# P's diagonal blocks filled by ScalarE, attention's queries turned during retention, and a new entry into the MLP

## The chip, the cores and the metric

The kernel runs on one core of a Trainium2 chip. Its engines are TensorE (PE for the matmuls, PEld for the loading of their stationary operand), VectorE (DVE), ScalarE (ACT), GpSimd (POOL) and SyncE (SP, which here issues the DMAs). The metric is the device time of one execution in microseconds; the time before is the median of three runs.

## The reference, cut to what matters

One decoder layer over 16 meta tokens and 1024 tokens of 1024 channels, in float32:

```python
u = rmsnorm(h, norm1_w); proj = u @ w_in
y_ret = retention(...)            # 4 heads, chunks of 128 tokens, state carried from chunk to chunk
score = sum_h iw[h] * relu(iq[h] @ ik.T)          # indexer, causal
sel = top_k(score, 256)                           # keys that a query may see
logits = (rmsnorm(q) / 8) @ rmsnorm(k)[sel].T + rel_bias[t5_bucket(dist)]
y_dsa = softmax(logits) @ v[sel]                  # 8 heads of 64, keys and values shared
h = h + concat(y_ret, y_dsa) @ w_out
h = h + square(relu(rmsnorm(h, norm2_w) @ w_ff1)) @ w_ff2     # 4096 wide
```

## The kernel before

Products are made in split precision: an operand is kept as a rounded high part and the low part that is left, and a product takes three matmuls (high by high, low by high, high by low). A high part is a ScalarE copy, a low part a subtract of the high part from the source, on VectorE or GpSimd. Much of the work off TensorE is this splitting.

The program goes through these stages. First come norm, transposes and the indexer's scores, block by block of 128 tokens (to about 205 us). Then retention runs head by head, eight chunks each (`ret_in`, `ret_out`), while the thresholds of the top 256 are searched bit by bit: tiles 2 to 4 by counting on VectorE (L746), tiles 5 to 7 by a sum of signs on ScalarE (L751). When a threshold is known, `masks` turns a score tile into a mask on VectorE (L761 to L767). From about 410 to 607 us attention goes through sixteen units, a block of 128 queries and a half of the heads each: `attend_p` makes the logits and the exponentials, `attend_v` transposes them, splits them and multiplies them by the values, and the first half of the output projection is laid between the units (`out_piece`). The second half of the output projection follows, with the second norm (`norm2`) between its blocks, and from about 664 us the MLP, whose two products are done by a scheme of seven products for a two by two split (units m = 1 to 7 over operands U1 to U7; `unit1`, then `stage2`).

The order in which each engine gets its instructions is not that of the program text: a planner orders all instructions by program position and by when it believes their inputs and buffers to be there, so work of a later part fills gaps of an earlier one. PSUM has eight banks, three of tag A (`psA`) and five of tag R (`psB`).

What the change touches:

- `load_q(i)` (L554): loads the normed queries of block i, turns them by four transposes, and splits them into the tile `qs`, whose 128 partitions hold high and low parts of two heads by turns. It takes two ScalarE copies (L565) and two VectorE subtracts (L566) a block.
- `attend_v` (L607): the meta tokens' few columns of the exponentials go into `pm`, which is zero outside its diagonal blocks of 32 partitions. A ScalarE copy (L618) gives the high part `hi`, and four VectorE instructions (L621), one for each block of 32 partitions, write high or low parts into `pm`. One matmul (L638) reads `pm` at the end of the unit.
- `norm2` (L876): norm, eight transposes, and then the operands U2 and U4 (from blocks 0 to 3) or U3, U5, U6, U7 and the sum for U1 (from blocks 4 to 7), each split into halves; the low halves of U3, U4 and U6 are made by GpSimd (`halves`, L895).
- `prep1`, `unit1`, `EVAC`, `groups` (L944 to L1024): a unit of the MLP's first product is 12 matmuls of 512 columns into one PSUM bank; EVAC says into which sums its result goes. Units run in groups; a group is a slice p of the MLP's width and some of the seven m. The first groups are p = 1 with m = 2 and 4, all of p = 0, and the rest of p = 1.
- the loop over `todo` (L1143 to L1156): the last output block of the first half, then eight of the second, whose weights are loaded and split by `out_w(1)` ahead of the first of these.

Of the kernel before, what the change touches and what calls it, by code (L numbers as in the profile page):

```python
# [22 lines left out]
NB = 8  # L23
# [58 lines left out]
def layer(ctx, tc, x, meta, norm1_w, w_in, ret_w, q_w, k_w, rel, w_out, norm2_w, w1, w2,  # L82
# [361 lines left out]
    qd = dr.tile([128, NB, 512], F32, name="qd")  # L444

# [108 lines left out]
    def load_q(i):  # L554
        qr = wp.tile([128, 512], F32, tag="rl", name="qr", bufs=2)
        nc.sync.dma_start(qr, qd[:, i])
        tp = psA()
        for c in range(4):
            nc.tensor.transpose(tp[:, 128 * c:128 * c + 128], qr[:, 128 * c:128 * c + 128], ident)
        qst[i] = at["q"][:, i % 2]  # L560
        t4 = tp.rearrange("p (c n) -> p c n", c=4)
        q4 = qst[i].rearrange("p (c e) n -> p c e n", e=2)
        for e in range(2):
            a, z = (slice(0, 64), slice(64, 128)) if e == 0 else (slice(64, 128), slice(0, 64))
            nc.scalar.activation(q4[a, :, e], t4[a], AF.Copy)  # L565
            nc.vector.tensor_tensor(q4[z, :, e], t4[a], q4[a, :, e].bitcast(F32), op=ALU.subtract)  # L566

# [39 lines left out]
    def attend_v(i, g):  # L607
# [9 lines left out]
        hi = small.tile([128, 128], F32R, name="phm", tag="ytmp", bufs=1)  # L617
        nc.scalar.activation(hi, tp[:, :128], AF.Copy)  # L618
        for hh in range(4):
            z = slice(32 * hh, 32 * hh + 32)  # L620
            nc.vector.scalar_tensor_tensor(pm[z, hh], tp[z, :128], odd[z], hi[z].bitcast(F32),  # L621
                                           op0=ALU.mult, op1=ALU.subtract)
# [102 lines left out]
    for h in range(4):  # L725
        st["w", h] = load_cols(w_in, [(o + 128 * h, 128) for o in (RQ, RK, RV, RG)])
        ret_meta(h)
        for c in range(NB):
            if h == 3 and c == 5:
                open_att()  # L730
                load_q(0)
            if h == 3 and c == 6:
                load_q(1)
            if h == 3 and c == 7:
                spread((4, attend_p(0, 0)))
            cur = ret_in(h, c)
            if prev:
                ret_out(*prev)
            prev = cur
# [136 lines left out]
    def norm2(b, src, u):  # L876
# [15 lines left out]
        def halves(m, x, eng):  # L892
            h, l = [v[:, :, s] for v in U[m]]
            nc.scalar.activation(h, x, AF.Copy)
            eng.tensor_tensor(l, x, h.bitcast(F32), op=SUB)  # L895
# [3 lines left out]

        def total(m, x, y, op, eng):  # L900
            t = temp()
            nc.vector.tensor_tensor(t, x, y, op=op)
            halves(m, t, eng)
        g1, g2 = f1[0][:, b % 4], f1[1][:, b % 4]
        if b < 4:
            nc.scalar.activation(g1, tps[0], AF.Copy)
            halves(2, tps[0], nc.vector)
            nc.scalar.activation(g2, tps[1], AF.Copy)
            total(4, tps[1], g1, SUB, nc.gpsimd)
        else:  # L910
            t = temp()
            nc.scalar.activation(t, tps[0], AF.Copy)
            total(3, t, tps[1], SUB, nc.gpsimd)
            halves(5, tps[1], nc.vector)
            total(6, tps[0], g1, ADD, nc.gpsimd)
            total(7, tps[1], g2, ADD, nc.vector)
            nc.vector.tensor_tensor(g1, tps[1], g1, op=ADD)

# [27 lines left out]
    EVAC = {2: [("1b", 1), ("2b", -1)], 4: [("1b", "+"), ("1a", 1)], 3: [("2a", 1), ("2b", "+")], 5: [("2a", "+"), ("1a", "-")],  # L946
            6: [("2b", "+")], 7: [("1a", "+")], 1: [("1a", "+"), ("2b", "+")]}
    FIN = {("1b", 4), ("2a", 5), ("1a", 1), ("2b", 1)}
    ORD = (2, 4, 3, 5, 6, 7, 1)
    groups = [(1, ORD[:2]), (0, ORD), (1, ORD[2:])] + [(p, ORD) for p in range(2, NP)]  # L950
# [43 lines left out]
    def unit1(n):  # L994
# [10 lines left out]
        for q, how in EVAC[m]:  # L1005
            if how in (1, -1):
                tag, k = ("yd", 4) if q in ("1a", "2b") else ("aop", 6)
                C[p, q] = p2["p"].tile([128, 512], F32, tag=tag, name="c" + q, bufs=k)
                nc.scalar.activation(C[p, q], ps, AF.Copy, scale=float(how))
            else:  # L1010
                c = C[p, q]
                nc.vector.tensor_tensor(c, c, ps, op=ADD if how == "+" else SUB)
                if (q, m) in FIN:
                    nc.scalar.activation(c, c, AF.Relu)
                    nc.scalar.activation(c, c, AF.Square)
                    if q in HELD:
                        nc.sync.dma_start(hid[HELD[q]][:, p], c)
# [126 lines left out]
    pre = out_prep(*todo[0])  # L1144
    for k, (ch, b) in enumerate(todo):
        if k == 1:
            out_w(1, True)
        nxt = out_prep(*todo[k + 1]) if k < NB else None
# [5 lines left out]
        if k == 6:  # L1154
            w1_load(0, 0)
            w1_load(0, 1)  # L1156

    for n in range(2):
        prep1(n)
# [5 lines left out]
    for n in range(len(units)):  # L1165
# [4 lines left out]
        if 3 <= n < 7:  # L1170
            s = slice(128 * (n - 3), 128 * (n - 3) + 128)
            nc.scalar.activation(U[1][0][:, :, s], f1[0][:, n - 3], AF.Copy)
            nc.vector.tensor_tensor(U[1][1][:, :, s], f1[0][:, n - 3], U[1][0][:, :, s].bitcast(F32), op=SUB)
# [48 lines left out]
```

## Time and profile before

| | |
|---|---|
| median of 3 runs | 1297.18 us (1294.48 to 1297.89) |
| the profiled execution | 1296.34 us, its span 1294.6 us, mean granted TensorE clock 0.989 |
| busy, share of the span | PE 96%, PEld 79%, VectorE 79%, ScalarE 59%, GpSimd 17% |
| the chain that ended last | PE 69%, VectorE 19%, ScalarE 5%, issue 4%, DMA 2%, GpSimd 1% |

Busy time of PE counts each matmul from its start to its end, and matmuls overlap, so that a stretch in which PE is 90% busy can still hold much less than 90% of the matmuls that would fit. The chain is followed back from the last instruction to what released each; a share of it is time that nothing else hid.

### The profile page before, as it was taken

The page shows a single profiled execution, that of the slowest core. Times are in us where ns is not written, and L with a number is a line of the kernel's source. Part 1 is how long each engine was busy: PE and PEld are TensorE (multiplying, and loading weights), DVE is VectorE, ACT ScalarE, POOL GpSimd, SP SyncE. Part 2 cuts the span into 40 slices and gives each one's busy share as a digit, 9 for nine tenths or more (in the row PEclk, how much of TensorE's full clock was granted, in tenths as well). Part 3 has the DMA queues.
Part 4 walks back from the last instruction along what each step waited for, and adds up shares of the span by engine and source line. Part 5 has one row for each costly group of instructions (what it writes and reads, how often), then busy time and mean ns, then how long its engine had stood idle before and what let it go on. Part 6 is the DMA issues. An engine that isn't in the chain of part 4 may idle for free.

```text
span 1294.6 us, 18365 instructions
## 1 busy us (share of the span) xinstructions
PE 1240.1 (96%) x6032; PEld 1025.8 (79%) x6032; DVE 1022.2 (79%) x2298; ACT 757.9 (59%) x1612; POOL 221.1 (17%) x278
## 2 busy tenths in 40 slices
PE   5999989999999899999898999999999999999998
PEld 4888868887887667877776888888888888888887
DVE  5579999993478899876489777777788887887875
ACT  6567567889956677665356555454565444444442
POOL 4003262424425322101241000000000200000000
PEclk8999999999999999999998999999999999999999
DMA  8103031202113223114953444344539835344222
GB/s 282 60 17 93 25 114 40 73 9 74 58 33 97 91 84 105 69 63 145 321 189 116 149 173 145 130 153 151 176 134 355 341 114 187 122 163 166 91 94 98
DMA packets 101279, 165.06 MB, mean 128 GB/s; under 512 B 8712, under 2 KB 48944, under 8 KB 97472
## 3 DMA queue, kind: packets, MB, share of 16 engines
q1 hardware_dynamic: 101184, 163.90, 36.7%
q8 instruction: 47, 0.77, 0.2%
q14 instruction: 48, 0.39, 0.1%
HBM read 113.46 MB, written 51.85 MB: 128 GB/s over the span
## 4 chain that ended last, share of the span: by engine, by line
PE 69%; DVE 19%; ACT 5%; issue 4%; DMA 2%; POOL 1%; SPq 0%; DVEq 0%; ACTq 0%
PE psB L1120 5%; PE psB L1121 5%; PE psB L1122 5%; PE psB L1002 4%; PE psB L1003 4%; PE psB L1004 4%; PE psA L1003 4%; PE psA L1002 4%; PE psA L1004 4%; DVE jk_cnt L746 3%; PE psA L246 3%; PE psA L247 3%; PE psA L248 3%; PE psA L1120 3%; PE psA L1121 3%
## 5 line engine op out<-in xcount | busy, mean ns | idle before, releaser
L973 ACT ACTIVATE wh<-ga 128x512 fp32r<-128x512 f32 x144 | 87.2, 628 | 159.2 <-PE psB L1121 138.3
L246 PE MATMUL psA<-wh,uh 128*128 128x512 f32 x376 | 150.3, 400 | 1.3 <-DVE fg L488 1.3
L247 PE MATMUL psA<-wh,ul 128*128 128x512 f32 x376 | 149.3, 397 | 0.0
L248 PE MATMUL psA<-wl,uh 128*128 128x512 f32 x376 | 149.1, 397 | 0.0
L974 DVE TENSOR_TENSOR wl<-ga,wh 128x512 fp32r<-128x512 f32 x144 | 96.6, 687 | 47.8 <-ACT wh L973 47.2
L973 ACT ACTIVATE wh<-sum 128x512 fp32r<-128x512 f32 x128 | 78.7, 625 | 79.2 <-DVE sum L970 70.9
L1121 PE MATMUL psB<-wh,wl 128*128 128x512 f32 x280 | 108.9, 389 | 0.0
L1122 PE MATMUL psB<-wl,wh 128*128 128x512 f32 x280 | 108.9, 389 | 0.0
L751 ACT ACTIVATE jk_top<-sc,tcand 128x784 bf16<-128x784 f32 (+2 forms) x93 | 98.3, 1057 | 14.9 <-DVE tcand L821 12.5
L1120 PE MATMUL psB<-wh 128*128 128x512 f32 x280 | 106.8, 389 | 0.0
L974 DVE TENSOR_TENSOR wl<-sum,wh 128x512 fp32r<-128x512 f32 x128 | 88.5, 693 | 4.0 <-ACT wh L973 4.0
L246 PEld LDWEIGHTS psA<-wh,uh 128*128 128x128 f32 x376 | 70.8, 188 | 14.0 <-issue 1.1
L248 PEld LDWEIGHTS psA<-wl,uh 128*128 128x128 f32 x376 | 70.8, 188 | 13.3
L247 PEld LDWEIGHTS psA<-wh,ul 128*128 128x128 f32 x376 | 71.1, 189 | 12.2
L1040 POOL COPY ga<-wl 128x1 f32<-128x1 f32 x8 | 6.6, 828 | 402.6 <-DVE wl L974 359.2
L746 DVE TENSOR_SCALAR_CACHE_REDUCE jk_cnt<-sc,tcand 128x400 bf16<-128x400 f32 (+2 forms) x93 | 70.4, 757 | 1.0
L359 ACT ACTIVATE rl<-psB,absw 128x320 f32<-128x320 f32 (+5 forms) x104 | 52.9, 555 | 28.0 <-DVE sc L363 13.9
L1121 PE MATMUL psA<-wh,wl 128*128 128x512 f32 x168 | 65.4, 389 | 0.0
L1122 PE MATMUL psA<-wl,wh 128*128 128x512 f32 x168 | 65.4, 389 | 0.0
L1120 PE MATMUL psA<-wh 128*128 128x512 f32 x168 | 64.9, 389 | 0.0
L194 POOL TENSOR_TENSOR wl<-wr,wh 128x512 fp32r<-128x512 f32 x44 | 60.3, 1390 | 19.2 <-ACT wh L189 13.9
L633 ACT ACTIVATE ph<-psB 128x512 fp32r<-128x512 f32 x72 | 41.4, 594 | 34.9 <-PE psB L628 26.8
(391 smaller groups left out, 3559.0 us busy)
## 6 DMA issues: line engine op xcount, KB each, us to landing
ga<-hid SPq DMA_DIRECT2D x28, 1024.0 KB, 5.2
wr<-in_w_ff_dram SPq DMA_DIRECT2D x34, 512.0 KB, 5.1
hid<-hs SPq DMA_DIRECT2D x48, 256.0 KB, 2.1
wr<-in_w_in_dram SPq DMA_DIRECT2D x32, 256.0 KB, 3.2
ysd<-ys SPq DMA_DIRECT2D x32, 256.0 KB, 2.8
ys<-ysd SPq DMA_DIRECT2D x32, 256.0 KB, 5.0
gb<-in_w_ff_dram SPq DMA_DIRECT2D x8, 1024.0 KB, 6.8
ga<-in_w_ff_dram SPq DMA_DIRECT2D x8, 1024.0 KB, 5.2
```

What stands on the lines that cost most here:

```text
L246: nc.tensor.matmul(ps[:P, :n], uh, wh, start=d == 0, stop=False)
L247: nc.tensor.matmul(ps[:P, :n], ul, wh, start=False, stop=False)
L248: nc.tensor.matmul(ps[:P, :n], uh, wl, start=False, stop=d == 7)
L746: nc.vector.tensor_scalar(jk_[:, :ncol[i]], sc[i], cand[:, j:j + 1], 0.0, op0=ALU.is_ge, op1=ALU.add, accum_out=cnt[:, j:j + 1])
L973: nc.scalar.activation(view(hi), s, AF.Copy)
L974: nc.vector.tensor_tensor(view(lo), s, view(hi).bitcast(F32), op=SUB)
L1002: nc.tensor.matmul(ps, hi[:, a], uh[:, d], start=d == 0, stop=False)
L1003: nc.tensor.matmul(ps, lo[:, a], uh[:, d], start=False, stop=False)
L1004: nc.tensor.matmul(ps, hi[:, a], ul[:, d], start=False, stop=d == 3)
L1120: nc.tensor.matmul(ps[tb], ah[:, t], bh, start=j == 0 and m not in CONT, stop=False, skip_group_check=True)
L1121: nc.tensor.matmul(ps[tb], al[:, t], bh, start=False, stop=False, skip_group_check=True)
L1122: nc.tensor.matmul(ps[tb], ah[:, t], bl, start=False, stop=j == NO - 1, skip_group_check=True)
```

## The change

The pieces `hi` and `pm` of `attend_v`: VectorE computes high minus or low part for all 128 partitions by one instruction, and ScalarE copies the four diagonal blocks into `pm`. `load_q` is cut in two: `turn_q(c)` loads, turns and splits the queries of a block during retention's third head (blocks 1 to 7) and at the start of the fourth (block 0), and writes the 512 KB result to device memory (`qsd`); `load_q(i)` is then one DMA. In `norm2` all low halves are made by VectorE; U7's halves, like U1's, are split off into `late_halves`, called between the units 5 to 8. The MLP's first units are m = 2 and 4 of p = 1 and of p = 2, and then p = 0; the evacuations of m = 2, 4 and 3 take one ScalarE copy each. In the loop over `todo` the weights of the second half are loaded by calls ahead of the loop and split group by group; the MLP's first weights are called for one block earlier, and its first two operands are prepared inside the loop.

```diff
+    qsd = dr.tile([128, NB, 8, 128], F32, name="qsd")
...
-    def load_q(i):
+    def turn_q(i):
         qr = wp.tile([128, 512], F32, tag="rl", name="qr", bufs=2)
         nc.sync.dma_start(qr, qd[:, i])
-        tp = psA()
+        tp = psB()
         for c in range(4):
             nc.tensor.transpose(tp[:, 128 * c:128 * c + 128], qr[:, 128 * c:128 * c + 128], ident)
-        qst[i] = at["q"][:, i % 2]
+        t = big.tile([128, 8, 128], F32R, tag="row", name="qt", bufs=3)
         t4 = tp.rearrange("p (c n) -> p c n", c=4)
-        q4 = qst[i].rearrange("p (c e) n -> p c e n", e=2)
+        q4 = t.rearrange("p (c e) n -> p c e n", e=2)
...
+        nc.sync.dma_start(qsd[:, i], t.bitcast(F32))
+
+    def load_q(i):
+        qst[i] = at["q"][:, i % 2]
+        nc.sync.dma_start(qst[i].bitcast(F32), qsd[:, i])
...
-        hi = small.tile([128, 128], F32R, name="phm", tag="ytmp", bufs=1)
-        nc.scalar.activation(hi, tp[:, :128], AF.Copy)
+        hi = small.tile([128, 2, 128], F32R, name="phm", tag="ytmp", bufs=1)
+        nc.scalar.activation(hi[:, 0], tp[:, :128], AF.Copy)
+        nc.vector.scalar_tensor_tensor(hi[:, 1], tp[:, :128], odd, hi[:, 0].bitcast(F32), op0=ALU.mult, op1=ALU.subtract)
         for hh in range(4):
             z = slice(32 * hh, 32 * hh + 32)
-            nc.vector.scalar_tensor_tensor(pm[z, hh], tp[z, :128], odd[z], hi[z].bitcast(F32),
-                                           op0=ALU.mult, op1=ALU.subtract)
+            nc.scalar.activation(pm[z, hh], hi[z, 1].bitcast(F32), AF.Copy)
...
+            if h == 2 and c:
+                turn_q(c)
+            elif h == 3 and c == 0:
+                turn_q(0)
...
         if b < 4:
             nc.scalar.activation(g1, tps[0], AF.Copy)
-            halves(2, tps[0], nc.vector)
+            halves(2, tps[0])
             nc.scalar.activation(g2, tps[1], AF.Copy)
-            total(4, tps[1], g1, SUB, nc.gpsimd)
+            nc.vector.tensor_tensor(t, tps[1], g1, op=SUB)
+            halves(4, t)
         else:
+            nc.scalar.activation(t, tps[0], AF.Copy)
+            nc.vector.tensor_tensor(t, t, tps[1], op=SUB)
+            halves(3, t)
+            halves(5, tps[1])
             t = temp()
-            nc.scalar.activation(t, tps[0], AF.Copy)
-            total(3, t, tps[1], SUB, nc.gpsimd)
-            halves(5, tps[1], nc.vector)
-            total(6, tps[0], g1, ADD, nc.gpsimd)
-            total(7, tps[1], g2, ADD, nc.vector)
+            nc.vector.tensor_tensor(t, tps[0], g1, op=ADD)
+            nc.vector.tensor_tensor(g2, tps[1], g2, op=ADD)
             nc.vector.tensor_tensor(g1, tps[1], g1, op=ADD)
+            halves(6, t)
+
+    def late_halves(m, tb):
+        s = slice(128 * tb, 128 * tb + 128)
+        h, l = [v[:, :, s] for v in U[m]]
+        x = f1[m == 7][:, tb]
+        nc.scalar.activation(h, x, AF.Copy)
+        nc.vector.tensor_tensor(l, x, h.bitcast(F32), op=SUB)
...
-    EVAC = {2: [("1b", 1), ("2b", -1)], 4: [("1b", "+"), ("1a", 1)], 3: [("2a", 1), ("2b", "+")], 5: [("2a", "+"), ("1a", "-")],
+    EVAC = {2: [("1b", "=")], 4: [("1a", "=")], 3: [("2a", "="), ("2b", "1b"), ("1b", "1a")], 5: [("2a", "+"), ("1a", "-")],
             6: [("2b", "+")], 7: [("1a", "+")], 1: [("1a", "+"), ("2b", "+")]}
-    FIN = {("1b", 4), ("2a", 5), ("1a", 1), ("2b", 1)}
+    FIN = {("1b", 3), ("2a", 5), ("1a", 1), ("2b", 1)}
...
-    groups = [(1, ORD[:2]), (0, ORD), (1, ORD[2:])] + [(p, ORD) for p in range(2, NP)]
+    groups = [(1, ORD[:2]), (2, ORD[:2]), (0, ORD), (1, ORD[2:]), (2, ORD[2:])] + [(p, ORD) for p in range(3, NP)]
...
+    def w_out_raw(g):
+        wraw[g] = wp.tile([128, 2, 512], F32, tag="wr", name="wr", bufs=3)
+        nc.sync.dma_start(wraw[g], w_out[256 * g:256 * g + 256, 512:].rearrange("(j p) w -> p j w", p=128))
...
+    for g in range(3):
+        w_out_raw(g)
     for k, (ch, b) in enumerate(todo):
         if k == 1:
-            out_w(1, True)
-        nxt = out_prep(*todo[k + 1]) if k < NB else None
+            ow[0] = [], []
+            for g in range(4):
+                if g == 1:
+                    nxt = out_prep(*todo[k + 1])
+                    w_out_raw(3)
+                w_out_split(g)
+        else:
+            nxt = out_prep(*todo[k + 1]) if k < NB else None
...
-        if k == 6:
+        if k == 5:
             w1_load(0, 0)
             w1_load(0, 1)
-
-    for n in range(2):
-        prep1(n)
+        if k in (6, 7):
+            prep1(k - 6)
...
-        if 3 <= n < 7:
-            s = slice(128 * (n - 3), 128 * (n - 3) + 128)
-            nc.scalar.activation(U[1][0][:, :, s], f1[0][:, n - 3], AF.Copy)
-            nc.vector.tensor_tensor(U[1][1][:, :, s], f1[0][:, n - 3], U[1][0][:, :, s].bitcast(F32), op=SUB)
+        for m, n0 in ((7, 5), (1, 7)):
+            if n == n0:
+                nc.gpsimd.tensor_copy(U[m][0][:, 0, 0:512:128], U[3][1][:, 0, 384:388].bitcast(F32))
+            for tb in (2 * (n - n0), 2 * (n - n0) + 1):
+                if 0 <= tb < 4:
+                    late_halves(m, tb)
```

## Rows read from the trace of the kernel before

**Rows 1.** Of the page: busy time of each engine, share of the span, instructions

```profile
PE 1240.1 (96%) x6032; PEld 1025.8 (79%) x6032; DVE 1022.2 (79%) x2298; ACT 757.9 (59%) x1612; POOL 221.1 (17%) x278
```

**Rows 2.** Windows: length, busy (count) PE, PEld, DVE, ACT, POOL; clock, DMA, GB/s

```profile
300.00:350.00 50.00, 49.44 (x254) 41.64 (x252) 16.17 (x71) 44.59 (x103) 15.45 (x26) 1.00 0.14 37
350.00:410.00 60.00, 58.80 (x313) 49.08 (x312) 45.79 (x112) 36.48 (x102) 23.74 (x39) 1.00 0.15 50
410.00:607.00 197.00, 180.92 (x1029) 145.98 (x1028) 166.48 (x575) 134.32 (x324) 43.09 (x27) 0.99 0.28 93
607.00:664.00 57.00, 53.35 (x246) 43.13 (x245) 31.18 (x38) 24.38 (x45) 15.31 (x22) 0.97 0.87 298
```

**Rows 3.** One stretch of the MLP, same columns

```profile
700.00:725.00 25.00, 25.00 (x112) 20.69 (x111) 21.16 (x35) 13.43 (x24) 0.00 (x0) 1.00 0.36 130
```

**Rows 4.** Chain that ended last between 410 and 607 us, shares by line

```profile
by line: DVE P L589 13.0%; DVE ph L634 9.2%; PE psB L628 8.4%; issue 7.1%; PE psB L695 7.1%; PE psB L696 6.5%; PE psB L694 6.2%; PE psB L636 5.2%; DVE pm L621 3.8%; ACT P L596 3.7%; ACT ph L633 3.6%; PE psB L635 3.5%; DVE qs L566 3.0%; PE p
```

**Rows 5.** Groups between 410 and 607 us: count, busy us, mean ns, idle before

```profile
L596 ACT ACTIVATE P<-P,m 128x272 f32<-128x272 f32 (+6 forms) x56 | 47.0, 839 | 10.5 <-DVE m L595 9.9 <-issue 0.2
...
L633 ACT ACTIVATE ph<-psB 128x512 fp32r<-128x512 f32 x72 | 41.4, 594 | 34.9 <-PE psB L628 26.8 <-PE psB L635 3.9 <-DVE ph L634 3.3
L628 PE MATMUL psB<-ident,P 128*128 128x128 f32 x288 | 41.4, 275 | 0.9 <-DVE pm L621 0.5 <-DVE ytmp L648 0.3
...
L621 DVE SCALAR_TENSOR_TENSOR pm<-psB,kss,phm 32x128 fp32r<-32x128 f32 x64 | 22.1, 346 | 2.1 <-ACT phm L618 1.4
...
L566 DVE TENSOR_TENSOR qs<-psA,qs 64x512 fp32r<-64x512 f32 x12 | 8.3, 688 | 0.6 <-ACT qs L565 0.3
...
L599 ACT ACTIVATE few<-P 128x64 f32<-128x64 f32 x30 | 7.1, 250 | 2.0 <-PE psB L616 1.8
L565 ACT ACTIVATE qs<-psA 64x512 fp32r<-64x512 f32 x12 | 7.1, 588 | 0.8 <-PE psA L559 0.4 <-DVE qs L566 0.3
...
L614 ACT ACTIVATE rx<-rs 128x256 f32<-128x256 f32 x15 | 6.2, 414 | 1.3 <-DVE m L595 0.5 <-DVE rs L602 0.4 <-PE psB L642 0.3
```

**Rows 6.** Chain that ended last, 300 to 350 and 350 to 410 us

```profile
by line: PE psA L246 28.1%; PE psA L247 27.6%; PE psA L248 27.5%; PE psB L506 3.1%; PE psB L500 3.1%; PE psB L502 2.7%; PE psB L507 2.2%; PE psB L495 1.5%; PE psB L496 1.5%; issue 0.6%; DVE fg L488 0.6%; PE psA L235 0.5%; PE psA L232 0.5%; 
...
by line: PE psA L246 13.0%; PE psA L248 12.6%; PE psA L247 12.6%; DVE cum L765 7.0%; DVE eq L766 4.1%; DVE eq L761 3.8%; issue 3.7%; DVE oh L517 3.6%; DVE qs L566 3.5%; ACT wh L189 3.0%; DVE eq L767 2.4%; DVE need L762 2.4%; DVE t L450 2.4%
```

**Rows 7.** ScalarE's costliest group between 300 and 350 us

```profile
L751 ACT ACTIVATE jk_top<-sc,tcand 128x784 bf16<-128x784 f32 (+2 forms) x32 | 33.7, 1054 | 4.2 <-DVE tcand L821 3.7
```

**Rows 8.** Entry of the MLP by stretch, columns as in the second group

```profile
666.20:690.60 24.40, 16.83 (x73) 12.87 (x71) 24.40 (x36) 16.61 (x31) 9.62 (x7) 0.86 0.36 117
676.40:682.50 6.10, 1.43 (x9) 0.87 (x9) 6.10 (x9) 3.76 (x8) 4.10 (x3) 0.83 0.88 265
687.70:690.60 2.90, 0.01 (x1) 0.00 (x0) 2.90 (x6) 2.86 (x6) 0.00 (x0) 1.00 0.06 21
690.60:694.20 3.60, 3.56 (x9) 2.84 (x10) 3.60 (x5) 2.69 (x5) 1.28 (x1) 0.53 0.19 73
661.20:690.60 29.40, 21.83 (x95) 16.96 (x94) 28.97 (x40) 21.61 (x40) 13.10 (x10) 0.88 0.38 121
```

**Rows 9.** VectorE's groups between 661.2 and 690.6 us

```profile
L974 DVE TENSOR_TENSOR wl<-sum,wh 128x512 fp32r<-128x512 f32 x6 | 5.0, 862 | 0.0
L881 DVE SCALAR_TENSOR_TENSOR un<-hrow,rs_y,nrow 128x1024 f32<-128x1024 f32 x2 | 4.6, 2320 | 0.0
```

**Rows 10.** Timeline of VectorE at 625 us and of GpSimd at 674 us

```profile
625.38 1.28 DVE L881 SCALAR_TENSOR_TENSOR un<-hrow,rs_y,nrow 128x1024 f32<-128x1024 f32 x1 [1.28 <-DMA ys<-ysd]
...
674.28 2.80 POOL L895 TENSOR_TENSOR u3l<-ut,u3h 128x512 fp32r<-128x512 f32 x1 [0.32 <-ACT u3h L894]
```

**Rows 11.** Pieces of the chain that ended last, in order of time

```profile
631.92 0.87 PE psB L889 x8
...
671.74 1.20 DVE wl L974 x2
```

**Rows 12.** A stretch ahead of the MLP, columns as in the second group

```profile
616.00:618.00 2.00, 0.52 (x3) 0.30 (x2) 0.44 (x1) 1.10 (x2) 0.00 (x0) 1.00 0.96 337
```

More of the change, by code (lines that the diff above doesn't have):

```diff
@@ L890, in norm2, with halves @@
             tps.append(tp)
-        def halves(m, x, eng):
+        def halves(m, x):
             h, l = [v[:, :, s] for v in U[m]]
             nc.scalar.activation(h, x, AF.Copy)
-            eng.tensor_tensor(l, x, h.bitcast(F32), op=SUB)
+            nc.vector.tensor_tensor(l, x, h.bitcast(F32), op=SUB)
         def temp():
             return p2["p"].tile([128, 4, 128], F32, tag="yd", name="ut", bufs=4)
[L900 to L903, printed above, removed]
         g1, g2 = f1[0][:, b % 4], f1[1][:, b % 4]
+        t = temp()
         if b < 4:
             nc.scalar.activation(g1, tps[0], AF.Copy)
-            halves(2, tps[0], nc.vector)
+            halves(2, tps[0])
             nc.scalar.activation(g2, tps[1], AF.Copy)
-            total(4, tps[1], g1, SUB, nc.gpsimd)
-        else:
+            nc.vector.tensor_tensor(t, tps[1], g1, op=SUB)
+            halves(4, t)
+        else:
+            nc.scalar.activation(t, tps[0], AF.Copy)
+            nc.vector.tensor_tensor(t, t, tps[1], op=SUB)
+            halves(3, t)
+            halves(5, tps[1])
             t = temp()
-            nc.scalar.activation(t, tps[0], AF.Copy)
-            total(3, t, tps[1], SUB, nc.gpsimd)
-            halves(5, tps[1], nc.vector)
-            total(6, tps[0], g1, ADD, nc.gpsimd)
-            total(7, tps[1], g2, ADD, nc.vector)
-            nc.vector.tensor_tensor(g1, tps[1], g1, op=ADD)
+            nc.vector.tensor_tensor(t, tps[0], g1, op=ADD)
+            nc.vector.tensor_tensor(g2, tps[1], g2, op=ADD)
+            nc.vector.tensor_tensor(g1, tps[1], g1, op=ADD)
+            halves(6, t)
[4 more added lines that the diff above has]
+        nc.scalar.activation(h, x, AF.Copy)
+        nc.vector.tensor_tensor(l, x, h.bitcast(F32), op=SUB)
     spread((NB + 1, attend_v(NB - 1, 1)), (9, out_piece(0, 6)))
@@ L1005, in unit1 @@
         for q, how in EVAC[m]:
-            if how in (1, -1):
-                tag, k = ("yd", 4) if q in ("1a", "2b") else ("aop", 6)
+            if (p, q) not in C:
+                tag, k = ("yd", 4) if q[0] == "2" else ("aop", 6)
                 C[p, q] = p2["p"].tile([128, 512], F32, tag=tag, name="c" + q, bufs=k)
-                nc.scalar.activation(C[p, q], ps, AF.Copy, scale=float(how))
+            c = C[p, q]
+            if how == "=":
+                nc.scalar.activation(c, ps, AF.Copy)
+            elif how == "1b":
+                nc.vector.tensor_tensor(c, ps, C[p, how], op=SUB)
+            elif how == "1a":
+                nc.vector.tensor_tensor(c, c, C[p, how], op=ADD)
             else:
-                c = C[p, q]
                 nc.vector.tensor_tensor(c, c, ps, op=ADD if how == "+" else SUB)
[L1013 to L1017, printed above, removed]
+            if (q, m) in FIN:
+                nc.scalar.activation(c, c, AF.Relu)
+                nc.scalar.activation(c, c, AF.Square)
+                if q in HELD:
+                    nc.sync.dma_start(hid[HELD[q]][:, p], c)
         if m == 1:
@@ L1144, in layer, with w_out_split @@
     pre = out_prep(*todo[0])
+    wraw = {}
+    def w_out_raw(g):
+        wraw[g] = wp.tile([128, 2, 512], F32, tag="wr", name="wr", bufs=3)
+        nc.sync.dma_start(wraw[g], w_out[256 * g:256 * g + 256, 512:].rearrange("(j p) w -> p j w", p=128))
+    def w_out_split(g):
+        for j in range(2):
+            d = 2 * g + j
+            for v, k in zip(split(wraw[g][:, j], 512, True, rgain[:, d:d + 1] if d < 4 else None), range(2)):
+                ow[0][k].append(v)
+    for g in range(3):
+        w_out_raw(g)
     for k, (ch, b) in enumerate(todo):
         if k == 1:
-            out_w(1, True)
-        nxt = out_prep(*todo[k + 1]) if k < NB else None
+            ow[0] = [], []
[6 more added lines that the diff above has]
+            nxt = out_prep(*todo[k + 1]) if k < NB else None
         spread((8, out_mm(ch, b, *pre)), *([(1.3, norm_step(b - 1))] if k >= 2 else []))
```

## The prediction

> **What bounds the kernel now.** I read the page first: PE is busy nearly everywhere, VectorE most of the time, GpSimd little [rows 1]. The MLP shows what a full PE is: 112 matmuls of 512 columns in 25 us, 0.2232 us each [rows 3], and a transpose of 128 columns takes 0.87/8 = 0.109 us [rows 11]. Nothing is to be won there; what counts is where PE waits ahead of it. So I read the windows by stage, then the chain of each.
>
> Attention, 410 to 607 us, is the largest. VectorE is busy 166 of 197 us and ScalarE 134; PE's 181 busy us hold overlapped matmuls only [rows 2]. The chain's costliest line there is VectorE's, and the two that the change touches, L621 and L566, hold 3.8% and 3.0% of it [rows 4], 7.5 and 5.9 us. Between 300 and 350 us, in retention, the chain is PE's for 98% (the sum of its PE lines) and VectorE is two thirds idle, but ScalarE is busy 44.6 of 50 us with the sign counts; from 350 to 410 us the masks on VectorE come onto the chain [rows 2, 6, 7].
>
> At the entry of the MLP PE has nothing to do for most of 676.4 to 682.5 us and all of 687.7 to 690.6 us, while VectorE is never idle, and until 694.2 us it has half the clock, 1.2 of 2.4 GHz [rows 8]. From 666.2 us, the end of the last output block, to 690.6, where U3 of block 7 comes, lie four units (p = 1 and 0, m = 2 and 4) and 24 transposes: 48 x 0.2232 + 24 x 0.109 = 13.3 us of work in 24.4 us. That is 11.1 us lost [rows 3, 8, 11]. At half clock the last stretch ran 9 matmuls in 3.6 us instead of 2.0, another 1.6 us: 12.7 us in all.
>
> **Attention.** Sixteen times four VectorE instructions of 346 ns go, 22.1 us; twelve subtracts of 688 ns go, 8.3 us, and twelve ScalarE copies, 7.1 us, with 24 transposes [rows 5]. On the chain that removes 7.5 + 5.9 = 13.4 us. What comes: sixteen VectorE instructions of 128 columns; I take 346 ns for each, as the old form has the same columns on fewer partitions, 5.5 us, of which the old share of L621 (7.5/22.1) is on the chain: 1.9 us. And 64 ScalarE copies of 128 columns from SBUF. No row shows that one; 64 columns take 250 ns and 256 take 414 [rows 5], so it lies between; on their line 305 ns, 19.5 us. ScalarE's two big groups have (3.7% + 3.6%) of 197 = 14.4 us of their 88.4 on the chain [rows 4, 5], 16%, so the copies add 3.1 us and the copies that go give back 1.1. L628's transposes have 16.5 us of the chain for 288, so 24 give 1.4. Sum: 13.4 - 1.9 - 3.1 + 1.1 + 1.4 = 11 us gained. Behind the old waits the next late thing is the copy and the split of the exponentials (L633, L634), which PE waits for. Bounds: nothing, if these chains are as long as the one removed, and 20 us, if all of VectorE's net 22.1 + 8.3 - 5.5 = 25 us less ScalarE's share of 5 is on the chain. The copies into `pm` wait for VectorE's instruction, and what stands behind them on ScalarE, the next copies for PE, waits too; I count that within these bounds. `load_q`'s DMA waits on SP for its half of `qs`, with attention's loads and stores behind it, but is called two units ahead, some 25 us (197/8), so I give it nothing; without that cover each of six loads would cost its transfer.
>
> The Trainium skill, in ScalarE: Activation LUTs, Rules for kernel authors, speaks against this part: additions and products belong on VectorE. Its section What ACT_TABLE_LOAD costs gives 186 ns + 0.833 ns a column, an estimate of 293 ns for this copy, by which the term of 3.1 would be 3.0.
>
> **Retention.** 32 transposes come, 3.5 us, on a PE that is the chain; eight of them (0.9 us) were there for blocks 0 and 1, so +2.6. VectorE's new subtracts lie in its idle time. Of L566, 3.5% of 60 us, 2.1 us, leaves the chain between 350 and 410 us [rows 6]. ScalarE gets 14 copies of 588 ns, 8.2 us, in the third head, where it has 5.4 us free in 50 [rows 2], so the sign counts end later, and with them the masks, which then push into attention's start. This I bound by 0 (retention's tail covers it) and 8.2, and take 3.5, near the 2.8 that don't fit: 2.6 - 2.1 + 3.5 = 4 us lost, between 0.5 and 8.7. The eight stores of 512 KB and the loads find the DMA 14% used [rows 2]; behind them on SP stand the next head's weights, called half a head ahead.
>
> **The MLP's entry.** Two more units that need only U2 and U4 put 24 x 0.2232 = 5.4 us of PE work ahead of U3: 666.2 + 13.3 + 5.4 = 684.9. When is U3 there? From 661.2 to 690.6 VectorE was busy 28.97 us with 40 instructions [rows 8]. Instructions of 512 columns follow each other in 0.60 us [rows 11]. Two each of U7's low halves, U1's low halves and the additions into 1b leave this stretch: -3.6. GpSimd no longer runs beside it: the norm's multiply took 2.32 us on average here [rows 9] against 1.28 alone, while GpSimd's subtract took 2.80 [rows 10], and six subtracts took 0.86 against the 0.69 of L566: -2.1 - 1.0. Seven low halves come from GpSimd (U3 and U6 of three blocks, U3 of the last): +4.2. The two added units' three preparations, 1.8 us, can be done before, in a stretch where VectorE is busy 31.2 of 57 us [rows 2]. Net -2.5, and U3 is there at 688.1, 3.2 us after PE needs it. With the 1.6 us at half clock, 4.8 of 12.7 stay: 8 us gained. Bounds: 0, if the planner's order keeps U3 late, and 12.7.
>
> On this the Trainium skill says, in SBUF — State Buffer, Who interferes with whom, that a VectorE instruction with two SBUF inputs and a GpSimd one that reads SBUF exclude each other. The rows of 1.28 and 2.32 us agree with it. By it each of the six GpSimd subtracts in this stretch could have held VectorE for its whole length; at 1.28 us each, an estimate, this relief would be 7.7 instead of 3.1.
>
> **At nothing.** The weights of the second half: three of four loads had landed long before, since their first copies ran without a wait, and the fourth needs a buffer that the first split frees. The loss there (PE 0.52 busy of 2 us at 616) stands beside a DMA at 0.96 [rows 12], and the edit moves no bytes; without cover it could lose or gain 3 us. One more reload of p = 2 is 1 MB, 3 us of the DMA, under the MLP. The evacuations give ScalarE one copy less in sixteen slices, but PE is full there and ScalarE busy 13 of 25 us [rows 3]; U7 and U1 are due three and four units after U3, 8 us or more (3 x 12 x 0.2232), for eight pairs of instructions of 0.6.
>
> The sum: 1296.3 - 11 + 4 - 8 = 1281.3 for the profiled execution; the median stands 0.84 higher, so 1282.
>
> **The rivals.** A: ScalarE takes what VectorE gives. For it: 19.5 - 7.1 = 12.4 us go onto an engine that is busy 134 of 197; against it: it is still the less busy one. Attention gains nothing: 1293. The Trainium skill's rule on ScalarE, named above, would lead here.
> B, the other side: a bank of PSUM. `turn_q` takes one of the five psB banks and keeps it until ScalarE and VectorE have read it twice, and ScalarE's queue is full of rounds of three sign counts of 1.05 us [rows 7], 3.2 us a round. If PE, which needs these banks for every chunk, stands for a round at each of eight turns, 25 us go: 1282 + 25 = 1307. It turns the change slower from 2.4 us a turn (19/8). Against it: between 300 and 350 us the chain hardly leaves PE, so banks are not short now.
> C: the entry does not get what it is made for. VectorE was the bound there, and it takes over seven subtracts from GpSimd; if the order still places U3 of block 7 at the end, nothing is won: 1290.
>
> **How the numbers follow.** The forecast has 0.62, A 0.15, C 0.12, B 0.11. No change within 0.3% (1293.3 to 1301.1), about what this measurement can tell, takes half of A (0.07), some of C and of the forecast's upper end (0.05). Slower is B and a rest: 0.11. Faster is what is left, 0.77. The forecast's own range goes from 1270 (attention at 20, entry near 12) to 1290; with A and C it reaches 1295, and leaves out B and the far low end, about 0.18.
>
> **What would show it.** L621 as 16 instructions near 0.35 us, 64 copies near 0.3 us on ScalarE; attention some 11 us shorter, with VectorE under 145 us busy; retention's end later by about 4 us; PE's holes between 676 and 691 us down to one of about 3 us, the norm's multiply back at 1.28 us, and U3 of block 7 used about 22 us after the last output block with six units ahead of it, where it now comes after 24.4 us with four. It is wrong if ScalarE becomes the engine that PE waits for in attention, if PE waits for ScalarE during the third head, or if PE's holes ahead of U3 still add up to 11 us.

## The result and the profile after

The changed kernel takes 1389.7 us (median of four runs, 1388.3 to 1391.5) against 1296.3 us (1294.5 to 1297.9), a ratio of 1.072 [1.070, 1.074]. It is 93 us slower, where 14 us faster was predicted.

The page of the changed kernel shows the place: in the slices from about 450 to 555 us PE hardly works, and its granted clock falls to 1.2 GHz with it.

```profile
span 1389.7 us, 18414 instructions
...
PE   6999989999994002999999999999999999999998
...
ACT  6575653124589884888654655555455444444442
...
PEclk9999999999996555999999999999999999999999
```

ScalarE's row, in which the sign counts lie, is low where it was full before (busy 44.6 of 50 us from 300 to 350 [rows 2]) and full where PE stands. The same by windows of the changed kernel:

```profile
core 0: us, PE busy (x) PEld busy (x) DVE busy (x) ACT busy (x) POOL busy (x), PEclk, DMA share, GB/s
200.00:375.00 175.00, 174.38 (x921) 147.26 (x920) 112.71 (x346) 60.99 (x184) 59.84 (x96) 1.00 0.25 78
375.00:450.00 75.00, 51.77 (x259) 43.23 (x257) 46.01 (x172) 65.57 (x178) 26.14 (x30) 0.81 0.23 74
450.00:525.00 75.00, 0.00 (x0) 0.00 (x0) 12.19 (x59) 60.86 (x106) 0.35 (x2) 0.50 0.00 0
525.00:550.00 25.00, 3.87 (x16) 3.73 (x17) 20.68 (x41) 9.34 (x18) 0.91 (x4) 0.50 0.03 11
```

So ScalarE is two thirds idle from 200 to 375 us, and the sign counts come afterwards, with nothing for PE to do beside them. The stage lengths put a number on it. Each is taken from the start of the last matmul of one stage to that of the next, in one profiled execution of each kernel (the experiments in the last four columns are told below):

| us | before | after | turned queries in another buffer | turned queries alone, so buffered | P's blocks alone | entry alone |
|---|---|---|---|---|---|---|
| end of retention | 418.0 | 421.4 | 427.8 | 428.4 | 418.2 | 417.9 |
| attention | 188.2 | 294.1 | 177.6 | 179.1 | 184.9 | 188.7 |
| output projection | 59.6 | 58.4 | 57.3 | 57.6 | 58.1 | 56.8 |
| MLP, first product | 319.9 | 306.9 | 306.8 | 319.8 | 319.7 | 306.7 |
| the rest | 308.9 | 308.9 | 309.0 | 308.9 | 308.9 | 309.0 |
| span | 1294.6 | 1389.7 | 1278.5 | 1293.8 | 1289.8 | 1279.1 |

A figure of this table is of a single execution: three kernels that leave attention as it was (the entry alone and two forms of it) have 187.2 to 188.7 us for it, so differences of 1 or 2 us say little.

Of the 95.1 us between the two profiled executions, +105.9 lie in attention, and all of it is one wait. This is the view of PE's waits of the changed kernel between 420 and 560 us:

```profile
engine line waited for: us in total, times, longest us
PE psB L635 <- DVE yd L656: 112.8, 1, 112.8
```

Three links lead back from it. **First**, the tiles. The next rows are single lines of the changed kernel's program, each with its count, durations (shortest, median, longest) and first and last start: the copy into the turned queries `qt`, tile 1's negation, the sign counts, and the signs of tile 1's mask.

```profile
L567 ACT ACTIVATE qt<-psB x16: 573/592/594, 313.8 to 367.4; 64x512 fp32r<-64x512 f32 x16
L789 ACT ACTIVATE neg<-sc x1: 429/429/429, 366.5 to 366.5; 128x272 f32<-128x272 f32 x1
L762 ACT ACTIVATE jk_top<-sc,tcand x93: 932/1054/1178, 203.5 to 519.0; 128x784 bf16<-128x784 f32 x31, 128x912 bf16<-128x912 f32 x31, 128x1040 bf16<-128x1040 f32 x31
L771 ACT ACTIVATE jk_top<-sc,tfew x1: 523/523/523, 370.8 to 370.8; 128x272 bf16<-128x272 f32 x1
```

The same lines in the kernel before:

```profile
L778 ACT ACTIVATE neg<-sc x1: 433/433/433, 75.3 to 75.3; 128x272 f32<-128x272 f32 x1
L751 ACT ACTIVATE jk_top<-sc,tcand x93: 932/1057/1197, 203.0 to 365.4; 128x784 bf16<-128x784 f32 x31, 128x912 bf16<-128x912 f32 x31, 128x1040 bf16<-128x1040 f32 x31
L760 ACT ACTIVATE jk_top<-sc,tfew x1: 522/522/522, 206.7 to 206.7; 128x272 bf16<-128x272 f32 x1
```

The negation `neg` (L789) of tile 1, whose scores are there early, moved from 75.3 to 366.5 us. `neg`, the masks' `cum` and now `qt` all take one of three buffers with the tag `row`. In the program text the eight `turn_q` stand in the retention loop and the search behind it, so `neg` comes ninth for these buffers, though `qt` does not need one before 313.8 us. **Second**, the junk tile. The mask of tile 1 throws its signs into `jk_top` (L771), the tile that the sign counts of tiles 5 to 7 write (L762). By the round robin over the searches it stands, in program order, behind the first bit of these counts and ahead of the second. ScalarE's timeline in the changed kernel shows the pair, first bit at 203 us and nothing more of it until the mask at 370.8 us is through:

```profile
203.45 0.95 ACT L762 ACTIVATE jk_top<-sc,tcand 128x784 bf16<-128x784 f32 x1
...
205.83 1.17 ACT L762 ACTIVATE jk_top<-sc,tcand 128x1040 bf16<-128x1040 f32 x1
...
370.78 0.52 ACT L771 ACTIVATE jk_top<-sc,tfew 128x272 bf16<-128x272 f32 x1 [2.83 <-DVE tfew L796]
...
371.92 0.93 ACT L762 ACTIVATE jk_top<-sc,tcand 128x784 bf16<-128x784 f32 x1
```

**Third**, the memory of the stage. `yd` (L656), which PE waits for, needs nothing of the masks as data. Its pool is opened behind the closing of the pool that holds `eq`, `cum` and `row`, in the same memory. (PE's transposes at L635 need no data of `yd`; by the program both work on banks of psB, and `yd` reads one out.) The timeline of the changed kernel has `yd` start 0.03 us after the last mask's copy ends (544.55 + 1.07), with VectorE idle for the 1.20 us of that copy:

```profile
544.55 1.07 ACT L779 ACTIVATE sc<-eq 128x1040 f32<-128x1040 bf16 x1 [6.58 <-DVE eq L778]
545.65 0.42 DVE L656 TENSOR_TENSOR yd<-psB,ytmp 128x256 f32<-128x256 f32 x1 [1.20 <-ACT sc L779]
```

The parts that the change is made of did what they were to do, behind this wait: the MLP's first product is 13.0 us shorter.

### The profile page after: what moved, and what is told of

It reads as the page before. It is cut to its first block, busy times and chain, and to the rows that moved or that the text cites. A ratio compares the mean times of both kernels' runs of the same rounds, so it can differ in the third digit from the quotient of the medians.

```text
span 1389.7 us, 18414 instructions
## 1 busy us (share of the span) xinstructions
PE 1236.7 (89%) x6032; PEld 1028.6 (74%) x6032; DVE 1011.9 (73%) x2262; ACT 776.0 (56%) x1660; POOL 202.5 (15%) x268
## 4 chain that ended last, share of the span: by engine, by line
PE 69%; DVE 15%; ACT 10%; issue 3%; DMA 2%; POOL 0%; SPq 0%; ACTq 0%; DVEq 0%; POOLq 0%
ACT jk_top L762 6%; PE psB L1146 5%; PE psB L1144 5%; PE psB L1145 5%; PE psA L246 4%; PE psA L247 4%; PE psA L248 4%; PE psA L1021 4%; PE psA L1023 4%; PE psA L1022 4%; PE psB L1023 4%; PE psB L1021 3%; PE psB L1022 3%; DVE jk_cnt L757 3%; PE psA L1146 3%
## 5 line engine op out<-in xcount | busy, mean ns | idle before, releaser
L635 PE MATMUL psB<-ident,P 128*128 128x128 f32 x288 | 42.1, 280 | 113.8 <-DVE yd L656 112.8
L635 PEld LDWEIGHTS psB<-ident,P 128*128 128x128 f32 x288 | 35.8, 145 | 119.6 <-DVE yd L656 113.0
L762 ACT ACTIVATE jk_top<-sc,tcand 128x784 bf16<-128x784 f32 (+2 forms) x93 | 98.0, 1054 | 18.0 <-DVE tcand L832 16.4
L246 PEld LDWEIGHTS psA<-wh,uh 128*128 128x128 f32 x376 | 71.0, 189 | 11.8 <-issue 0.2
```

Of the source, the lines that this page charges most:

```text
L246: nc.tensor.matmul(ps[:P, :n], uh, wh, start=d == 0, stop=False)
L762: nc.scalar.activation(jk_top[:, :ncol[i]], sc[i], AF.Sign, scale=-1.0, bias=cand[:, j:j + 1], accum_out=cnt[:, j:j + 1])
```

## Experiments

The theory: three small tiles in a row (`row` buffers given out in program order, the junk tile, the memory of the stage) hold attention up. The rivals were those of the prediction: ScalarE overloaded by the new copies, a bank of PSUM held by the turning, or a part that is slow by itself. All ratios are to the kernel before, with their 95% intervals.

### The turned queries in another buffer

```diff
-        t = big.tile([128, 8, 128], F32R, tag="row", name="qt", bufs=3)
+        t = const.tile([128, 8, 128], F32R, tag="nrow", name="qt")
```

(The load of `nrow2`, whose memory this is, moves behind the retention loop.)

> The whole change, but the turned queries of `turn_q` use the memory of the constant row `nrow2` (its load moved behind retention) and no longer a buffer of the tag `row`. Theory R (the sign counts of tiles 5 to 7 wait for the junk tile of tile 1's mask, and this mask waits for a `row` buffer behind the eight turned tiles): tile 1's negation is back before 100 us, the second bit of the sign counts follows the first within 10 us, the last mask ends near 405 to 415 us, and the kernel takes 1275 to 1295 us. Rival B (a PSUM bank held by the turning) or rival A (ScalarE overloaded by the new copies): nothing of this moves and the time stays at 1380 to 1395 us.

Measured: 1279.9 us, ratio 0.9874 [0.9860, 0.9889]. One buffer in the place of three, and 110 us are back. The same two lines in this kernel:

```profile
L789 ACT ACTIVATE neg<-sc x1: 432/432/432, 76.2 to 76.2; 128x272 f32<-128x272 f32 x1
...
L762 ACT ACTIVATE jk_top<-sc,tcand x93: 932/1057/1173, 203.9 to 372.6; 128x784 bf16<-128x784 f32 x31, 128x912 bf16<-128x912 f32 x31, 128x1040 bf16<-128x1040 f32 x31
```

Every other instruction of the change is still there, the bank and ScalarE's copies too, so the rivals can't account for these 110 us.

### The second link by itself

```diff
+        jk_ = eq if jk_ is None else jk_
...
-        masks(i, T, jk_top)
+        masks(i, T, None)
```

> The whole change, but the mask of tile 1 writes its unused signs into its own tile `eq` and not into the junk tile that the sign counts share. The buffers of `row` are as in the change. Theory R: tile 1's negation stays near 366 us, but the sign counts run from about 205 us on, their masks end by about 415 to 430 us, and the kernel takes 1280 to 1310 us. If the late `row` buffers cost the time by themselves, and not through the junk tile: 1370 us or more.

Measured: 1292.2 us, 0.9974 [0.9962, 0.9987]. The negation is later still than in the change, the sign counts are not:

```profile
L790 ACT ACTIVATE neg<-sc x1: 430/430/430, 379.9 to 379.9; 128x272 f32<-128x272 f32 x1
...
L762 ACT ACTIVATE jk_top<-sc,tcand x93: 932/1057/1202, 203.1 to 370.3; 128x784 bf16<-128x784 f32 x31, 128x912 bf16<-128x912 f32 x31, 128x1040 bf16<-128x1040 f32 x31
```

Without the junk tile 97 of 110 us are back (1389.7 to 1292.2), and the late buffers by themselves cost the other 12, as the masks end at 441 us here and at 405 with the other buffer. The third link was not tried apart. Here the first `yd` starts at 442.7 us, 1.6 us after the last mask's copy ends and just behind its own input `ytmp`, so this trace neither shows the link nor speaks against it. It rests on the program's text and on the traces of the two slow kernels, the change and the turned queries alone (below), where `yd` follows that copy within 0.03 us. In both, the masks' instructions also stand ahead of `yd` in VectorE's order, which by itself would have held it until 1.2 us earlier; so what the memory adds to the order is not shown.

### Program order or too few buffers

Tile 1's search and mask (and with them the functions that hold them) are written ahead of the retention loop; buffers and work stay as they are.

```diff
+    few1 = top_few(1)
+    next(few1)
+    for _ in few1:
+        pass
     prev = None
     for h in range(4):
...
-    runs = [top_few(1), topk([2, 3, 4], False), topk([5, 6, 7], True)]
+    runs = [topk([2, 3, 4], False), topk([5, 6, 7], True)]
```

> The whole change, with the search and the mask of tile 1 written in the program ahead of retention, so that its `row` buffers come ahead of the turned queries in program order; the number of buffers (3) and all the work stay the same. If buffers of a tag are given out in program order (theory R): tile 1's mask is done before 110 us, the sign counts run from about 205 us, and the time is 1275 to 1310 us. If three buffers are simply too few for turned queries and masks together: the sign counts stay late and the time stays above 1350 us.

Measured: 1286.2 us, 0.9923 [0.9907, 0.9940]. The negation and the sign counts are back in their places:

```profile
L755 ACT ACTIVATE neg<-sc x1: 431/431/431, 75.1 to 75.1; 128x272 f32<-128x272 f32 x1
...
L801 ACT ACTIVATE jk_top<-sc,tcand x93: 932/1057/1198, 203.1 to 373.1; 128x784 bf16<-128x784 f32 x31, 128x912 bf16<-128x912 f32 x31, 128x1040 bf16<-128x1040 f32 x31
```

The three buffers are enough; their order was wrong. The 6 us that are lost to the first experiment go with the other masks, which still come behind the turned queries: the last of their copies starts at 423.7 us, with the other buffer at 404.3.

### Each part alone

The turned queries alone, in the `row` buffers of the change:

> The kernel before with `turn_q` and the short `load_q` alone; P's blocks and the MLP's entry stay as they were. Theory R: 1380 to 1405 us, with PE standing for about 100 us ahead of the first `yd`. If the loss comes from the ScalarE copies into `pm` or from the entry: 1285 to 1300 us.

Measured: 1405.3 us, 1.0847 [1.0831, 1.0863]. PE's waits between 420 and 560 us:

```profile
PE psB L635 <- DVE yd L656: 111.4, 1, 111.4
```

This part alone makes the change slow. The rest without it:

> The whole change without `turn_q`: P's blocks by ScalarE and the MLP's new entry, the queries turned in attention as before. By the terms of the prediction: 2.5 us for the blocks (7.5 - 1.9 - 3.1) and 8 us for the entry, so a ratio near 0.992 (1286 us). If the order in which buffers are given out is the only thing that made the change slower, no stage ends later than in the kernel before. Rival A (ScalarE takes what VectorE gives) and rival C (the entry gains nothing) would each take their term away: 0.994 and 0.998.

Measured: 1279.4 us, 0.9875 [0.9860, 0.9890], and no stage ends later. P's blocks alone:

> The kernel before with P's diagonal blocks by ScalarE alone. By the terms of the prediction 2.5 us less, a ratio of 0.998 and attention shorter by that. Rival A: ScalarE's 64 copies (about 19.5 us in attention) take it back, ratio 1.000 or above.

Measured: 1293.4 us, 0.9981 [0.9973, 0.9990]; attention 3.3 us shorter. Rival A falls. The entry alone:

> The kernel before with the MLP's new entry alone (the low halves all on VectorE, the late halves, the two units of p = 2 ahead, the new evacuations, the weights by groups). By the prediction's term 8 us less, a ratio near 0.994, bounds 0 and 12.7 us; the norm's multiply at 1.28 us and one hole of PE of about 3 us ahead of U3. Rival C: ratio 1.000.

Measured: 1280.9 us, 0.9888 [0.9874, 0.9901]. Rival C falls, and the gain is nearly twice the term. The turned queries alone, in the other buffer:

> The kernel before with the turned queries alone, written into the memory of `nrow2` and not into `row` buffers. By the terms of the prediction: attention gains 5.9 + 1.1 + 1.4 = 8.4 us, retention loses 4 us, so 4.4 us less, a ratio of 0.997; the same edit with `row` buffers took 1405 us. If a PSUM bank or ScalarE in retention costs more than that (rival B, up to 25 us): 1.000 to 1.015.

Measured: 1295.7 us, 1.0006 [0.9994, 1.0018]. Attention gains 9.1 us, retention loses 10.4 (the table above), so with a good buffer this part is worth nothing. This is not the border between the two stages moving: ahead of retention's last matmul PE has run 11 of the logits' high matmuls (L594) here, and 10 (L587) in the kernel before. That is why the change with the other buffer (0.9874) and the change without this part (0.9875) are the same.

### What the turning costs retention

High parts copied by VectorE instead of ScalarE, on top of the other buffer:

```diff
-            nc.scalar.activation(q4[a, :, e], t4[a], AF.Copy)
+            nc.vector.tensor_copy(q4[a, :, e], t4[a])
```

> The whole change with the turned queries in the memory of `nrow2` and their high parts copied by VectorE, not ScalarE. In the run with ScalarE's copies and the same memory the last sign count came 7.2 us later than in the kernel before and retention's last matmul 9.8 us later. If ScalarE's queue in the third head is what costs this: the sign counts end within 2 us of the kernel before, retention's end is 4 to 7 us earlier than with ScalarE's copies, and the ratio falls from 0.987 to about 0.983. If the turned queries' transposes, loads or bank cost it, retention's end stays within 2 us of 427.8 us and the ratio at 0.987.

Measured: 1277.7 us, 0.9848 [0.9827, 0.9868], the fastest kernel of this study; its interval overlaps that of the first experiment. Groups of lines and windows of this kernel:

```profile
L567 DVE CAST qt<-psB 64x512 fp32r<-64x512 f32 x16 | 11.0, 688 | 4.8 <-DMA qsd<-qt 2.5 <-PE psB L508 2.1
...
300.00:350.00 50.00, 50.00 (x268) 42.55 (x268) 29.35 (x85) 41.25 (x92) 11.91 (x22) 1.00 0.28 95
```

Retention ends at 422.6 us, 5.2 earlier than with ScalarE's copies, as the first theory had it (this profiled execution, 1274.8 us, is the fastest of its four, so the 5.2 may flatter). But its mechanism doesn't hold: ScalarE has 41.3 busy us in place of 46.8 from 300 to 350 us, and the sign counts' last start is at 372.9 us, no earlier than 372.6. A bit of the count passes through ScalarE and VectorE by turns, and VectorE now has 29.4 busy us there, 16.2 before [rows 2].

Six of the eight blocks turned in the fourth head, two at the end of the third:

> The whole change with the turned queries in the memory of `nrow2`, six of the eight turned in the fourth head, where the sign counts are over from about 366 us, and two at the end of the third. If ScalarE's queue beside the sign counts costs the time: sign counts end 5 us earlier than with all turns in the third head, and the ratio falls to about 0.983. If the cost only depends on the number of turns, the ratio stays at 0.987; if the masks on VectorE are the tighter place, it is 0.990 or above.

Measured: 1282.7 us, 0.9887 [0.9869, 0.9906]. The sign counts' last start is at 369.5 us, 3 us earlier, but the last mask's copy starts at 405.2 as with all turns in the third head, and retention ends at 431.7, 3.9 us later. The interval holds the value for "only the number of turns counts" and touches that of the masks. How the cost divides between the two engines' queues stays open; ScalarE's queue alone it is not. What PE's rows show of it stands below, under retention.

### Why the entry gained more

The entry alone, without the two units of p = 2 ahead (U7's and U1's late halves two units earlier):

```diff
-    groups = [(1, ORD[:2]), (2, ORD[:2]), (0, ORD), (1, ORD[2:]), (2, ORD[2:])] + [(p, ORD) for p in range(3, NP)]
+    groups = [(1, ORD[:2]), (0, ORD), (1, ORD[2:])] + [(p, ORD) for p in range(2, NP)]
```

> The MLP's new entry alone, without the two units of p = 2 ahead of p = 0 (U7's and U1's late halves two units earlier, so that they still come ahead of their use). The entry as a whole measured a ratio of 0.989, U3 of block 7 at 681.9 us, 18.5 us after the last output matmul. By the prediction, which has U3 ready at a time that VectorE sets and only counts the two units (5.4 us) as cover: 5.4 us of the gain go, ratio 0.993. If the shorter work of VectorE is what counts, and U3 comes before the units end: the ratio stays within 0.001 of 0.989.

Measured: 1290.0 us, 0.9943 [0.9924, 0.9962]. PE's waits from 664 to 700 us, and windows over the same place:

```profile
PE psB L1010 <- ACT u3h L894: 3.2, 1, 3.2
PE psB L1012 <- DVE u3l L895: 0.6, 1, 0.6
```

```profile
679.00:682.00 3.00, 0.32 (x1) 0.32 (x2) 3.00 (x6) 3.00 (x8) 0.00 (x0) 0.81 0.00 0
682.00:686.00 4.00, 3.41 (x8) 2.21 (x8) 4.00 (x8) 1.71 (x5) 0.38 (x2) 0.50 0.00 0
686.00:690.00 4.00, 4.00 (x10) 3.08 (x10) 4.00 (x8) 3.79 (x9) 0.00 (x0) 0.50 0.00 0
690.00:694.00 4.00, 4.00 (x17) 3.22 (x16) 4.00 (x7) 1.68 (x3) 0.00 (x0) 0.87 0.10 13
```

U3 comes 17.5 us after the last output matmul (681.7 - 664.2) with four units ahead of it, where the kernel before took 24.8 (690.6 - 665.8); the wait that is left costs 3.8 us and then 8 us at 1.2 GHz, in which 18 matmuls of 512 columns ran where 36 would fit. With the two units on top, U3 would be there before PE asks.

The entry alone, with the low halves of U3, U4 and U6 back on GpSimd:

```diff
-            nc.vector.tensor_tensor(l, x, h.bitcast(F32), op=SUB)
+            (nc.gpsimd if m in (3, 4, 6) else nc.vector).tensor_tensor(l, x, h.bitcast(F32), op=SUB)
```

> The MLP's new entry alone, but the low halves of U3, U4 and U6 made by GpSimd again, beside VectorE. By the prediction's terms (VectorE saves 3.1 us where GpSimd is quiet, and pays 4.2 us for seven subtracts): within 2 us of the entry as a whole, ratio 0.988 to 0.991. If GpSimd's subtracts (2.8 us each, and the norm's multiply at 2.32 in place of 1.28 us beside them) were what kept U3 late, 5 us or more of the gain go: 0.993 or above.

Measured: 1284.5 us, 0.9899 [0.9883, 0.9916], not to be told from the entry as a whole by the ratio. Groups of this kernel between 658 and 690 us:

```profile
L895 POOL TENSOR_TENSOR u3l<-ut,u3h 128x512 fp32r<-128x512 f32 x4 | 8.5, 2133 | 8.6 <-ACT u3h L894 8.6
L982 DVE TENSOR_TENSOR wl<-sum,wh 128x512 fp32r<-128x512 f32 x6 | 6.3, 1042 | 0.0
L895 POOL TENSOR_TENSOR u6l<-ut,u6h 128x512 fp32r<-128x512 f32 x4 | 5.6, 1407 | 0.0
...
L881 DVE SCALAR_TENSOR_TENSOR un<-hrow,rs_y,nrow 128x1024 f32<-128x1024 f32 x3 | 4.5, 1485 | 0.0
L982 DVE TENSOR_TENSOR wl<-wr,wh 128x512 fp32r<-128x512 f32 x5 | 4.4, 899 | 0.0
...
L978 DVE TENSOR_TENSOR sum<-wr 128x512 f32<-128x512 f32 x3 | 3.0, 999 | 0.0
```

VectorE's subtract takes 1042 ns on the mean beside GpSimd's, 690 without them (below). The first product of the MLP is 2.4 us longer than the entry's own (309.1 against 306.7 us). So in these single profiles the two units are worth 9.1 us (315.8 against 306.7; by the ratios, 0.9943 against 0.9888, 7 us) and VectorE's low halves 2.4, which the ratios can't tell from nothing.

## Why the prediction was wrong

**The step that failed** is the retention step, in its sentence on the late sign counts ("This I bound by 0 (retention's tail covers it) and 8.2, and take 3.5"). It counted ScalarE's copies, the transposes, the stores and, as rival B, a bank, but not the tile that the result goes into: `tag="row"`, shared with the masks and asked for ahead of them. The sign counts came 154 us late (519.0 against 365.4), not 3.5. No rival had it either; B was on the right side for a reason that isn't there, since with the other buffer the bank and the copies stay and the 110 us go. With the buffer changed, the kernel takes 1279.9 us where 1282 was forecast, but that is the sum of errors of both signs:

**Retention**, +4 predicted, bounds 0.5 to 8.7: +9.8 us with the other buffer (427.8 against 418.0). Mis-sized, beyond the bound: the last sign count starts 7.2 us later, where 3.5 was taken, and near the end of the stage PE stands and then runs at a lower clock, which the sum had at nothing. PE's longest wait there with the other buffer, and windows with the other buffer (first) and with VectorE's copies (second):

```profile
PE psB L508 <- DVE sm L505: 2.5, 1, 2.5
...
420.00:430.00 10.00, 7.60 (x35) 7.03 (x36) 7.62 (x30) 7.29 (x27) 5.45 (x6) 0.66 0.72 258
...
420.00:430.00 10.00, 8.70 (x59) 7.38 (x58) 8.48 (x50) 9.47 (x37) 6.17 (x5) 1.00 0.52 176
```

Ahead of `sm` VectorE has splits of the output weights (L196). Three of them take 5.1 us here, from 414.3 us on, and 2.4 with VectorE's copies; the group between 405 and 425 us in the two kernels:

```profile
L196 DVE SCALAR_TENSOR_TENSOR wl<-wr,rgain,wh 128x512 fp32r<-128x512 f32 x4 | 7.4, 1862 | 0.7 <-ACT wh L189 0.7
...
L196 DVE SCALAR_TENSOR_TENSOR wl<-wr,rgain,wh 128x512 fp32r<-128x512 f32 x4 | 3.2, 826 | 1.0 <-ACT wh L189 1.0
```

The wait of 2.5 us and some 3 us of clock (0.66 of 10 us) are of the size of the 5.2 us between these two ends of retention, and the mean clock over the four runs differs the same way (0.990 to 0.993, and 0.995 to 0.996). That they are the cause is argued from these rows; no run takes them apart.

**Attention**, -11: -10.6 us. Split as predicted too: 2.5 for P's blocks measured 3.3, 8.4 for the turned queries 9.1 (single profiles; the two don't add up to 10.6). Lines of `phm` and the window of attention in the kernel with the other buffer:

```profile
L629 ACT ACTIVATE pm<-phm x64: 289/307/312, 428.6 to 594.8; 32x128 fp32r<-32x128 f32 x64
...
L626 DVE SCALAR_TENSOR_TENSOR phm<-psB,kss,phm x16: 341/347/352, 427.3 to 593.5; 128x128 fp32r<-128x128 f32 x16
```

```profile
427.80:605.80 178.00, 169.90 (x961) 138.01 (x960) 135.15 (x491) 139.41 (x353) 37.20 (x21) 0.99 0.28 97
```

The copy that no row showed was put at 305 ns between two measured ones and takes 307; the Trainium skill's rate (ScalarE: Activation LUTs, What ACT_TABLE_LOAD costs), 293 by estimate, is 5% low. VectorE is busy 135 us, under the 145 named. ScalarE is now the busier of the two (139 us), and attention is still 3.3 us shorter with the copies alone, so rival A did not come. What went to ScalarE are copies; the product and the subtraction stayed on VectorE. PE's waits for VectorE in this stage fall from 11.8 us in sum to 5.1, those for ScalarE rise from 1.4 to 2.3, so the named sign, ScalarE as the engine that PE waits for, did not come either.

**The entry**, -8, bounds 0 and 12.7: -13.1 us. The mechanism was right, the size off: U3 was to come 3.2 us late and cost 1.6 us at half clock, and it came in time. The window from the last output matmul to U3, with the other buffer, and the norm's multiply there:

```profile
662.70:681.30 18.60, 18.60 (x92) 15.50 (x91) 17.89 (x29) 12.90 (x25) 5.13 (x4) 1.00 0.19 58
```

```profile
L993 DVE TENSOR_TENSOR wl<-sum,wh 128x512 fp32r<-128x512 f32 x6 | 4.1, 690 | 0.0
...
L993 DVE TENSOR_TENSOR wl<-wr,wh 128x512 fp32r<-128x512 f32 x4 | 2.7, 692 | 0.0
...
L892 DVE SCALAR_TENSOR_TENSOR un<-hrow,rs_y,nrow 128x1024 f32<-128x1024 f32 x2 | 2.6, 1284 | 0.7 <-POOL rs_y L142 0.7
L989 DVE TENSOR_TENSOR sum<-wr 128x512 f32<-128x512 f32 x3 | 2.1, 691 | 0.0
```

There is no hole, the clock stays at 2.4 GHz, and the multiply is back at 1.28 us, as predicted. The subtracts of the preparations, too, take 690 ns where [rows 9] show 862. From 4.6 us ahead of the last output matmul VectorE has 36 instructions up to U3, not the 41 that the prediction's terms make of [rows 8]: mainly because the subtracts of three preparations and two of U3's low halves lie outside this stretch. VectorE's relief by GpSimd's silence was put at 3.1 us, and at 7.7 by an estimate from the rule of the Trainium skill (SBUF — State Buffer, Who interferes with whom). The last experiment's rows agree that the two engines hold each other up. Between 658 and 690 us, beside eight GpSimd subtracts, four groups of VectorE are longer than the same groups without them: 6 x 0.35 + 5 x 0.21 + 3 x 0.31 + 3 x 0.2 = 4.7 us. That is 0.6 us for each GpSimd subtract, or 3.5 us for the six of the prediction's stretch, near the smaller figure. The means hide how it comes about: of these seventeen VectorE instructions five are held, by 0.6 to 1.1 us each (one subtract took 1775 ns where the median is 683), and the others not at all. At other meetings it is GpSimd's subtract that is long, up to 2.80 us where the shortest takes 1.30.

**At nothing**: the output projection is 2.3 us shorter, within the 3 us named, but also with P's blocks or the turned queries alone (1.5 and 2.0), so it isn't shown that the weights' new order does it.

## What to carry to other kernels

A moved step also moves its claim on every tile it writes: list the tag of each new tile, who else draws on it, and who is ahead in program order, and follow what those others write, down to tiles that nobody reads. Where buffers are given out in program order, a tile that is filled late should not share a tag with one that is due early, and a junk tile should belong to one chain alone. A part with gains and losses in different stages is worth a run by itself: the turned queries gained 9 us in one stage and lost 10 in the stage before.

## What was not expected of the hardware

After PE's wait of 3.2 us for U3 in the entry without the two units, the clock was granted at 1.2 GHz for the next 8 us (the windows from 682 to 690 us), with PE busy 3.4 and 4.0 of 4 us in them: half the speed cost 4 us after a wait of 3.8. Taking ScalarE's 16 copies away from the stretch of the sign counts did not bring their end forward (372.9 against 372.6 us).
